# Head, rope weights and first post-norm of a decoder layer: a row tile in halves, low parts moved to GpSimd, scalings moved to ScalarE

## The chip, the cores and the metric

The kernel runs on one core of a Trainium2 chip. The metric is the device time of one execution in microseconds. The time of a kernel is the median over several executions; the profile comes from one further execution, whose own time is given beside its span.

The engines are named as the profile names them: TensorE is PE (its weight load is a row of its own, PEld), VectorE is DVE, ScalarE is ACT, GpSimd is POOL, SyncE is SP. Each engine takes its instructions in a fixed order, and a transfer is issued by an instruction in the queue of an engine.

## The reference

One decoder layer on 512 tokens of width 1024, all in float32:

```python
h = layer_norm(x, ln_in_g, ln_in_b)
proj = h @ w_in                       # q, k, v, r, gate rank, latents, branch gates
y_gla = (rms_norm(gla_chunked(q, k, v, log_a)) * silu(r)) @ w_o_gla
qm = rms_norm(q_lat) @ w_q_b          # 8 heads, each 128 plain + 64 rope columns
y_mla = merge(mla_causal_attention(...)) @ w_o_mla
mix = (g_gla * y_gla + g_mla * y_mla) @ w_out
h = layer_norm(alpha * h + mix, ln1_g, ln1_b)
ff = square(relu(h @ w_ff1)) @ w_ff2
return layer_norm(alpha * h + ff, ln2_g, ln2_b)
```

## The kernel before

**Precision.** A float32 operand is split into a high part, rounded to the type fp32r, and a low part, the rest. ACT writes the high part and DVE subtracts it to get the low part (`split`, L103 to L110). Each product is three matmuls, high by high, high by low and low by high: L230 to L232 in `gemm_fm`, which gives an output with features on the partitions, and L263 to L265 in `gemm_tm`, which gives tokens on the partitions.

**Weights.** All weights go through one stream of entries of up to 1024 columns in total. For each entry SP issues the transfers into `wraw` (three buffers), ACT converts it into `whi` (L179) and DVE subtracts for `wlo` (L180); `whi` and `wlo` have two buffers each. `pump` keeps the transfers two entries ahead of the products and the conversion one entry ahead. `plan` cuts a weight into entries of `per` blocks of 128 rows, two unless said otherwise. For the entries of the latent projection (`lat`, marked `res`) the parts have the names `xh` and `xl`, and they are converted ahead of their turn.

**Head.** `x` comes in four row tiles of 128 tokens. `load_x` (L117) puts their transfers on SP's queue: tile 0 in two halves of 512 columns, then tile 1 whole, both ahead of the first weights, tiles 2 and 3 later. `ln_rows` (L345) takes the statistics of a row tile in two halves (L348, DVE), aggregates them, adds the epsilon (L350), raises to the power -0.5 on POOL (L351) and normalises. For tile 0 that is done on ACT (L355) with a bias `nmr` that DVE works out (L354); for the others on DVE (L357). `ln_transpose` (L359) then goes over the eight blocks of 128 features: PE transposes the block for a pair of row tiles into PSUM (L366, two transposes), ACT scales and shifts it and rounds it to the high part `h` (L369), a second scaling of the same block gives `lnt` in full precision, and DVE subtracts for the low part (L374). The second scaling is on DVE (L373), or, with `alt`, on ACT for odd blocks (L371). `ln_in0` does this for row tiles 0 and 1 with `alt`, `ln_in1` for 2 and 3 without. Behind the first pair of tiles come the latent products of those tokens, token-major, then the same for the second pair, then q and k.

`last_in` is the low part of one block of the first pair. Some small DVE work of the head may be issued only after it. `lane_levels` begins with two copies of the lane masks into `cmask` (L910, DVE), which the GLA levels use much later.

**Middle.** The GLA levels run as a side lane beside the projections of v, r and of the branch gates. The gates are two groups of projections, and after each one `mla_qr` multiplies the normalised latent with the rope columns of four heads: 64 columns of each head of `w_q_b`, 256 columns, three blocks of 128 rows. `plan_qr` (L290) plans these weights with `per` = 2, so there are two entries for each group, one of two row blocks and one of one. The next entry behind the second group is the first one of `w_o_gla` for `y_gla`.

**First post-norm (LN1).** Behind the output projection `ln1` runs `ln_rows` and `ln_transpose` (without `alt`, name `h1`) for one pair of row tiles after the other; the second pair runs beside the first products of `w_ff1`, which use the first pair's tokens only.

**What sets the order.** The kernel's text yields from many generators, and a scheduler with its own model of the costs then fixes the order of the instructions on each engine. `tc.issue_after(x)` forbids an instruction to be issued ahead of x. So an edit in one place can move instructions of others on an engine. The profile's lines are those of the kernel before.

Of the kernel before, what the change touches and what calls it, by code (L numbers as in the profile page):

```python
# [16 lines left out]
ALU = mybir.AluOpType  # L17
AX = mybir.AxisListType

P = 128  # L20
T = 512
D = 1024
# [9 lines left out]
NOPE = 128  # L32
ROPE = 64
HQ = NOPE + ROPE
# [12 lines left out]
LEVELS = (1, 2, 4, 8, 16, 32, 64)  # L47
# [5 lines left out]
def tile_hybrid_block(ctx: ExitStack, tc: tile.TileContext, I, out, dbg=None):  # L53
    nc = tc.nc
# [17 lines left out]
    def A(shape, dt=F32, n="a"):  # L72
        tag, bufs = ("C", 8) if n in TAG_C else (n, TAG_W[n]) if n in TAG_W else ("A", 24)
        return pa.tile(shape, dt, tag=tag, bufs=bufs, name=nm(n))

    def B(shape, dt=F32, n="b"):
        return pb.tile(shape, dt, tag="B", name=nm(n))

    def S(shape, dt=F32, n="s"):
        return sm.tile(shape, dt, tag=n, name=nm(n))  # L80

    def MM(n="mm"):
        return pm.tile([P, T], F32, tag="mm", name=nm(n))

    def PX(shape=(P, T), dt=F32, n="px"):
        return px.tile(list(shape), dt, tag="px", name=nm(n))

    def f(ap):
        return ap.bitcast(F32)

    act = nc.scalar.activation
    vtt = nc.vector.tensor_tensor
    vts = nc.vector.tensor_scalar
    stt = nc.vector.scalar_tensor_tensor
    gtt = nc.gpsimd.tensor_tensor
# [21 lines left out]
    def load_x(*tts):  # L117
        for tt in tts:
            t = A([P, D], F32, "x")
            for c in (slice(0, T), slice(T, D)) if tt == 0 else (slice(0, D),):  # L120
                nc.sync.dma_start(t[:, c], I["x"][tt * P:(tt + 1) * P, c])
            xt.append(t)
    load_x(0, 1)
    ident = ca[:, 0:P]
    g_in = ca[:, P:P + NK]
# [8 lines left out]
    st = {"dma": 0, "spl": 0, "gates": ()}  # L134
    DMA_AHEAD, SPLIT_AHEAD = 2, 1

    def plan(name, c0, n, k_lo=0, k_hi=None, heads=None, res=False, per=2):
        w = I[name]
        K = w.shape[0] // P
        k_hi = K if k_hi is None else k_hi  # L140
        idx = []
        for k0 in range(k_lo, k_hi, per):
            nk = min(per, k_hi - k0)
            if heads is None:
                src = w.rearrange("(k p) n -> p k n", p=P)
                dmas = [(slice(0, nk), src[:, k0:k0 + nk, c0:c0 + n], None)]
            else:
                hw, h0, nh = heads
                src = w.rearrange("(k p) (h c) -> p k h c", p=P, c=hw)
                cw = n // nh  # L150
                dmas = [(kk, src[:, k0 + kk, h0:h0 + nh, c0:c0 + cw], cw) for kk in range(nk)]
            idx.append(len(stream))
            stream.append({"dmas": dmas, "nk": nk, "n": n, "res": res})
        return {"idx": idx, "nk": k_hi - k_lo, "per": per}

    def pump(i):
        while st["dma"] < min(len(stream), i + 1 + DMA_AHEAD):
            e = stream[st["dma"]]
            st["dma"] += 1
            if "src" in e:  # L160
                continue
            raw = A([P, e["nk"], T * 2 // e["nk"]], F32, "wraw")
            for sl, src, cw in e["dmas"]:
                dst = raw[:, sl, :e["n"]]
                if cw is not None:
                    dst = dst.rearrange("p (h c) -> p h c", c=cw)
                nc.sync.dma_start(dst, src)
            e["raw"] = raw
        while st["spl"] < min(len(stream), i + 2 + SPLIT_AHEAD):
            e = stream[st["spl"]]  # L170
            if st["spl"] > i + e.get("ahead", SPLIT_AHEAD) and not e["res"]:
                break
            nk, n = e["nk"], e["n"]
            hi, lo = [A([P, nk, T * 2 // nk], F32R, w) for w in HOME["a" if e["res"] else e.get("home", "w")]]
            raw = e["src"]() if "src" in e else e.pop("raw")
            with ExitStack() as gates:
                for g in st["gates"]:
                    gates.enter_context(tc.issue_after(g.ins))
                st["ins"] = act(hi[:, :nk, :n], raw[:, :nk, :n], AF.Copy)  # L179
                vtt(lo[:, :nk, :n], raw[:, :nk, :n], f(hi[:, :nk, :n]), op=ALU.subtract)  # L180
            st["gates"] = ()
            e["w"] = (hi, lo)
            st["spl"] += 1
# [33 lines left out]
    def part(x, i, c):  # L217
        return x[i][:, c] if isinstance(x, tuple) else x[:, i, c]
# [63 lines left out]
    PL = {}  # L282
# [5 lines left out]
        PL["v", hp] = plan("w_in", C_V + hp * T, T)  # L288
        PL["r", hp] = plan("w_in", C_R + hp * T, T)
    def plan_qr(g):  # L290
        PL["qr", g] = plan("w_q_b", NOPE, 4 * ROPE, heads=(HQ, 4 * g, 4))

    for br in range(2):
        for mb in range(2):
            PL["g", br, mb] = plan("w_in", C_G + br * D + mb * T, T)
        plan_qr(br)
# [48 lines left out]
    def ln_rows(src, dst, mv, on_act=False):  # L345
        bst = S([P, 2, 6], F32, "bst")
        for j in range(2):
            nc.vector.bn_stats(bst[:, j, :], src[:, j * T:(j + 1) * T])  # L348
        nc.vector.bn_aggr(mv, bst)
        vts(mv[:, 1:2], mv[:, 1:2], LN_EPS, None, op0=ALU.add)  # L350
        st["pow"] = gtt(mv[:, 1:2], mv[:, 1:2], mhalf[:, 0:1], op=ALU.pow)  # L351
        if on_act:
            nmr = S([P, 1], F32, "nmr")
            stt(nmr, mv[:, 0:1], -1.0, mv[:, 1:2], op0=ALU.mult, op1=ALU.mult)  # L354
            act(dst, src, AF.Identity, scale=mv[:, 1:2], bias=nmr)  # L355
        else:
            vts(dst, src, mv[:, 0:1], mv[:, 1:2], op0=ALU.subtract, op1=ALU.mult)  # L357

    def ln_transpose(rows, g, b, outs, hf, alt=False, n="h0"):  # L359
        tk = slice(hf * 256, (hf + 1) * 256)  # L360
        for k in range(NK):
            if len(outs) <= k:
                outs.append(A([P, 2, T], F32R, n) if n == "h0" else (B([P, T], F32R, n), B([P, T], F32R, n)))
            p = MM() if alt and k in (4, 5) else PX()
            for i in range(2):
                nc.tensor.transpose(p[:, i * P:(i + 1) * P], rows[2 * hf + i][:, k * P:(k + 1) * P], ident)  # L366
            tmp = B([P, 256], F32, "lnt")
            hi, lo = part(outs[k], 0, tk), part(outs[k], 1, tk)
            ha = act(hi, p[:, :256], AF.Identity, scale=g[:, k:k + 1], bias=b[:, k:k + 1])  # L369
            if alt and k % 2:  # L370
                act(tmp, p[:, :256], AF.Identity, scale=g[:, k:k + 1], bias=b[:, k:k + 1])  # L371
            else:
                vts(tmp, p[:, :256], g[:, k:k + 1], b[:, k:k + 1], op0=ALU.mult, op1=ALU.add)  # L373
            hd = vtt(lo, tmp, f(hi), op=ALU.subtract)  # L374
            if n == "h1":
                st["ln"] = (ha, hd)
            yield hd
# [4 lines left out]
    def ln_in0():  # L382
        for tt in range(2):
            ln_rows(xt[tt], xt[tt], mvin[:, tt, :], on_act=tt == 0)
        yield from ln_transpose(xt, g_in, b_in, hT, 0, alt=True)

    pump(-1)
    last_in = list(ln_in0())[3]


    act(identr, ident, AF.Copy)
# [7 lines left out]
    lmask = cmask.bitcast(U8)[:, :nl * 256].rearrange("p (l o u i) -> p l o u i", l=nl, o=2, u=2)  # L399
    lmi = A([P, 2, len(LEVELS), 64], I32, "lmi")  # L400
# [395 lines left out]
    def mla_pair(pr):  # L796
        vt = [None] * NT
        qn = [None] * 2
        kn = [None] * 2

        def ev_v(a, j, ps):
            t = B([P, 2, 256], F32R, "mv")
            split(ps[:, :256], t[:, 0, :], t[:, 1, :])
            vt[a] = t

        def ev_n(dst, sc):
            def e(a, ps):
                dst[a] = A([P, 2, T], F32R, "qn")
                split(ps, dst[a][:, 0, :], dst[a][:, 1, :], scale=sc)
            return e  # L810
        gemm_fm(PL["qn", pr], qlT, 256, ev_n(qn, scale))
        gemm_fm(PL["kn", pr], ckT, 256, ev_n(kn, None))
        return ([spawn(mla_head(2 * pr + a, a, qn[a], kn[a], vt)) for a in range(2)],
                lambda guard=None: gemm_tm([PL["mv", pr]], ckT, 256, ev_v, guard=guard))
# [92 lines left out]

    def lane_levels():
        for o in range(2):
            nc.vector.tensor_copy(lmask[:, :, o], lmi[:, o, :, None, :].to_broadcast([P, len(LEVELS), 2, 64]))  # L910
        for h in range(GH):
            yield from gla_levels(h)
            lv[h] = True

    def lane_out():
        for h in range(GH):
            yield from gla_out(h)

    t_lv, t_out = spawn(lane_levels()), spawn(lane_out())

    def levels_upto(h):
# [56 lines left out]
    t0, mv = mla_pair(0)  # L978
    mv()
    y_gla(1)  # L980
    t1, mv = mla_pair(1)
    mv(lambda: finish(*t0))
    t2, mv = mla_pair(2)
    mv(lambda: finish(*t1))
    t3, mv = mla_pair(3)
# [322 lines left out]
```

## Time and profile before

| | |
|---|---|
| median of 3 runs | 889.64 us (889.6, 889.64, 890.25) |
| the profiled execution's own time | 889.94 us |
| its span in the trace | 888.0 us, 11561 instructions |
| granted TensorE clock, mean | 0.996 |
| PE busy | 866.7 us, 98% of the span, 4352 matmuls |
| PE weight load busy | 738.3 us, 83% |
| DVE busy | 578.2 us, 65% |
| ACT busy | 432.7 us, 49% |
| POOL busy | 173.8 us, 20% |

The share of busy time is over the whole span. A row of the timeline gives the start in us from the span's start, the duration of the group, the engine, line, operation, and output and inputs; in square brackets stands the idle time ahead of it and what ended that. `x4` at its end means that four equal instructions in a row are shown as one row. A row of the waits gives who waited, for whom, the sum in us, the count and the mean. A row of the windows gives the stretch, its length with PE's busy time and count, the granted clock, the share of the transfer engines and their GB/s.

### The profile page before, as it was taken

To read this page: it belongs to the slowest core of one execution; us is meant where nothing else is said; L and a number is where in the kernel's file an instruction comes from. 1 tells how busy PE (TensorE), PEld (TensorE's weight loads), DVE (VectorE), ACT (ScalarE), POOL (GpSimd) and SP (SyncE) were. 2 spreads that over 40 slices of the span, in tenths; PEclk is the share of its full clock that TensorE was granted. 3 is DMA by queue.
4 is the path that set the end of the run, shared out by engine and by line. 5 is a ranking of instruction groups with operands and counts; after the bars stand their busy time and mean duration, and the time that the engine had idled before them with its cause. 6 is when DMAs were issued, how large, how long until landed. Compare 5 with 4: busy or idle time off the path is not lost.

```text
span 888.0 us, 11561 instructions
## 1 busy us (share of the span) xinstructions
PE 866.7 (98%) x4352; PEld 738.3 (83%) x4352; DVE 578.2 (65%) x987; ACT 432.7 (49%) x734; POOL 173.8 (20%) x211
## 2 busy tenths in 40 slices
PE   5999999999999999999999999999999999999995
PEld 5988888888888888889888888988888888888884
DVE  7834875667735234657766797997557646754687
ACT  5446453445434334435654423466357546645661
POOL 0303441434512010000000012104400520242022
PEclk9999999999999999999999999999999999999998
DMA  7513223221223232111307628006940991398075
GB/s 231 147 48 90 77 72 95 72 72 48 78 59 88 74 107 91 61 46 55 102 25 277 190 70 286 1 0 158 296 117 25 258 254 31 70 308 192 1 189 95
DMA packets 63270, 101.13 MB, mean 114 GB/s; under 512 B 7761, under 2 KB 31748, under 8 KB 63216
## 3 DMA queue, kind: packets, MB, share of 16 engines
q1 hardware_dynamic: 48256, 64.04, 23.4%
q0 software_dynamic: 13040, 32.71, 15.3%
q10 hardware_dynamic: 1920, 3.66, 1.2%
q8 instruction: 34, 0.56, 0.2%
q14 instruction: 20, 0.16, 0.1%
HBM read 82.56 MB, written 3.67 MB: 97 GB/s over the span
## 4 chain that ended last, share of the span: by engine, by line
PE 95%; DVE 2%; DMA 2%; issue 1%; ACT 0%; POOLq 0%; SPq 0%; POOL 0%; DVEq 0%; ACTq 0%
PE mm L230 16%; PE mm L232 16%; PE mm L231 16%; PE mm L263 5%; PE mm L265 5%; PE mm L264 5%; PE px L1153 3%; PE px L1155 3%; PE px L1154 3%; PE mm L1153 2%; PE mm L1155 2%; PE mm L1154 2%; PE px L690 1%; DMA x<-in_x_dram 1%; PE px L852 1%; PE px L265 1%
## 5 line engine op out<-in xcount | busy, mean ns | idle before, releaser
L180 DVE TENSOR_TENSOR wlo<-wraw,whi 128x1024 fp32r<-128x1024 f32 (+1 forms) x104 | 117.4, 1129 | 152.8 <-ACT whi L179 147.6
L230 PE MATMUL mm<-h,whi 128*128 128x512 f32 x416 | 162.8, 393 | 0.0
L231 PE MATMUL mm<-h,whi 128*128 128x512 f32 x416 | 162.2, 390 | 0.0
L179 ACT ACTIVATE whi<-wraw 128x1024 fp32r<-128x1024 f32 (+1 forms) x104 | 100.2, 963 | 122.2 <-PE mm L231 62.9
L232 PE MATMUL mm<-h,wlo 128*128 128x512 f32 x416 | 155.3, 390 | 0.0
L1181 POOL DMA_DIRECT2D res<-ev x54 | 47.8, 989 | 236.2 <-ACT ev L1179 196.4
L232 PEld LDWEIGHTS mm<-h,wlo 128*128 128x128 f32 x416 | 78.1, 188 | 16.3
L230 PEld LDWEIGHTS mm<-h,whi 128*128 128x128 f32 x416 | 78.1, 188 | 15.6
L231 PEld LDWEIGHTS mm<-h,whi 128*128 128x128 f32 x416 | 78.1, 188 | 15.6
L264 PE MATMUL mm<-wlo,h 128*128 128x512 f32 x128 | 50.6, 395 | 0.0
L265 PE MATMUL mm<-whi,h 128*128 128x512 f32 x128 | 50.3, 394 | 0.0
L263 PE MATMUL mm<-whi,h 128*128 128x512 f32 x128 | 49.9, 400 | 0.0
L1235 ACT ACTIVATE relu<-mm 128x512 f32<-128x512 f32 x32 | 18.8, 595 | 57.3 <-PE mm L232 57.3
L351 POOL TENSOR_TENSOR mv<-mv,mhalf 128x1 f32<-128x1 f32 x4 | 5.5, 1385 | 209.2 <-DVE mv L350 209.2
L616 POOL TENSOR_TENSOR rp<-rp 128x256 f32<-128x256 f32 x32 | 29.9, 936 | 63.6 <-ACT E L634 52.8
L641 DVE TENSOR_TENSOR M<-E,qk 128x256 f32<-128x256 f32 x48 | 28.9, 629 | 12.4 <-ACT E L634 12.2
L634 ACT ACTIVATE E<-rp 128x512 f32<-128x512 f32 x32 | 20.4, 638 | 26.2 <-POOL rp L617 26.1
L179 ACT ACTIVATE xh<-wraw 128x1024 fp32r<-128x1024 f32 (+1 forms) x20 | 18.9, 959 | 26.9 <-PE mm L265 15.5
L180 DVE TENSOR_TENSOR wlo<-wq,whi 128x1024 fp32r<-128x1024 f32 x15 | 18.4, 1224 | 19.7 <-ACT whi L179 19.7
L265 PEld LDWEIGHTS mm<-whi,h 128*128 128x128 f32 x128 | 24.1, 188 | 4.8
L264 PEld LDWEIGHTS mm<-wlo,h 128*128 128x128 f32 x128 | 24.1, 188 | 4.5
L263 PEld LDWEIGHTS mm<-whi,h 128*128 128x128 f32 x128 | 24.0, 188 | 4.2
(381 smaller groups left out, 2235.2 us busy)
## 6 DMA issues: line engine op xcount, KB each, us to landing
wraw<-in_w_in_dram SPq DMA_DIRECT2D x40, 512.0 KB, 3.7
wraw<-in_w_ff_dram SPq DMA_DIRECT2D x32, 512.0 KB, 8.0
wq<-in_w_ff_dram POOLq DMA_DIRECT2D x32, 512.0 KB, 9.3
res<-ev POOLq DMA_DIRECT2D x54, 256.0 KB, 8.8
wraw<-in_w_o_gla_dram SPq DMA_DIRECT2D x8, 512.0 KB, 3.7
wraw<-in_w_o_mla_dram SPq DMA_DIRECT2D x8, 512.0 KB, 3.3
wraw<-in_w_out_dram SPq DMA_DIRECT2D x8, 512.0 KB, 4.2
wraw<-in_w_in_dram SPq DMA_DIRECT2D x8, 360.0 KB, 4.6
```

What stands on the lines that cost most here:

```text
L179: st["ins"] = act(hi[:, :nk, :n], raw[:, :nk, :n], AF.Copy)
L180: vtt(lo[:, :nk, :n], raw[:, :nk, :n], f(hi[:, :nk, :n]), op=ALU.subtract)
L230: mm(o, hi[:, c], xh, start=first, stop=False)
L231: mm(o, hi[:, c], xl, start=False, stop=False)
L232: mm(o, lo[:, c], xh, start=False, stop=last)
L263: mm(o, xh, hi[:, :n], start=opens, stop=False, skip_group_check=share)
L264: mm(o, xh, lo[:, :n], start=False, stop=False, skip_group_check=share)
L265: mm(o, xl, hi[:, :n], start=False, stop=last, skip_group_check=share)
L1153: mm(o, xh[:, c], hi[:, pp, cols], start=opens, stop=False, skip_group_check=True)
L1154: mm(o, xh[:, c], lo[:, pp, cols], start=False, stop=False, skip_group_check=True)
L1155: mm(o, xl[:, c], hi[:, pp, cols], start=False, stop=hf == 1 and pp == 1, skip_group_check=True)
L1181: nc.gpsimd.dma_start(res[tt + t][:, j * T:(j + 1) * T], e, accum_op=ALU.add)
```

## The change

There are four edits.

1. In the head, row tile 1 is loaded in two halves like tile 0. The second half's statistics of tile 1 may be issued only after tile 0's `nmr`.
2. In the head, for the four odd blocks of row tiles 0 and 1, where ACT does the second scaling, POOL subtracts for the low part instead of DVE. `last_in` becomes the low part of the fifth block instead of the fourth, and the two lane mask copies wait for it too.
3. A group's rope weights become one entry of three row blocks (`per` = 4). The three transfers stay as they are.
4. In LN1 the second scaling of odd blocks is done by ACT instead of DVE. The low part stays on DVE there.

```diff
-            for c in (slice(0, T), slice(T, D)) if tt == 0 else (slice(0, D),):
+            for c in (slice(0, T), slice(T, D)) if tt < 2 else (slice(0, D),):
                 nc.sync.dma_start(t[:, c], I["x"][tt * P:(tt + 1) * P, c])
...
     def plan_qr(g):
-        PL["qr", g] = plan("w_q_b", NOPE, 4 * ROPE, heads=(HQ, 4 * g, 4))
+        PL["qr", g] = plan("w_q_b", NOPE, 4 * ROPE, heads=(HQ, 4 * g, 4), per=4)
...
     def ln_rows(src, dst, mv, on_act=False):
         bst = S([P, 2, 6], F32, "bst")
         for j in range(2):
-            nc.vector.bn_stats(bst[:, j, :], src[:, j * T:(j + 1) * T])
+            with ExitStack() as after:
+                if j and "nmr" in st:
+                    after.enter_context(tc.issue_after(st.pop("nmr").ins))
+                nc.vector.bn_stats(bst[:, j, :], src[:, j * T:(j + 1) * T])
...
-            stt(nmr, mv[:, 0:1], -1.0, mv[:, 1:2], op0=ALU.mult, op1=ALU.mult)
+            st["nmr"] = stt(nmr, mv[:, 0:1], -1.0, mv[:, 1:2], op0=ALU.mult, op1=ALU.mult)
...
-            if alt and k % 2:
+            if k % 2 and (alt or n == "h1"):
                 act(tmp, p[:, :256], AF.Identity, scale=g[:, k:k + 1], bias=b[:, k:k + 1])
             else:
                 vts(tmp, p[:, :256], g[:, k:k + 1], b[:, k:k + 1], op0=ALU.mult, op1=ALU.add)
-            hd = vtt(lo, tmp, f(hi), op=ALU.subtract)
+            hd = (gtt if alt and k % 2 else vtt)(lo, tmp, f(hi), op=ALU.subtract)
...
-    last_in = list(ln_in0())[3]
+    last_in = list(ln_in0())[4]
...
         for o in range(2):
-            nc.vector.tensor_copy(lmask[:, :, o], lmi[:, o, :, None, :].to_broadcast([P, len(LEVELS), 2, 64]))
+            with tc.issue_after(last_in.ins):
+                nc.vector.tensor_copy(lmask[:, :, o], lmi[:, o, :, None, :].to_broadcast([P, len(LEVELS), 2, 64]))
```

## Prediction

> **What bounds the kernel now.** I read the page's head and its chain first, then who TensorE (PE) waited for, then the stretches, and last the timeline at each place where PE stood still.
>
> ```profile
> PE 95%; DVE 2%; DMA 2%; issue 1%; ACT 0%; POOLq 0%; SPq 0%; POOL 0%; DVEq 0%; ACTq 0%
> ```
> ```profile
> PE px L366 <- ACT x L355: 9.0, 1, 9.0
> ...
> PE mm L263 <- ACT h L369: 0.8, 1, 0.8
> ...
> PE mm L265 <- DVE h L374: 0.7, 1, 0.7
> ...
> PE mm L232 <- DVE wlo L180: 0.5, 1, 0.5
> ...
> PE mm L230 <- ACT h L369: 0.3, 1, 0.3
> ```
> ```profile
> 870.00:888.00 18.00, 8.18 (x47) 0.82 0.63 117
> ```
>
> 95% of the chain that ended last is PE. The second view is the waits of PE: 9.0 us before its first instruction, and four short ones, 2.3 us together. The third gives PE's busy time at the end: 8.18 of 18 us, so 9.8 us of tail. The change touches no matmul and no instruction of the tail. It can only shorten the start, the four waits and what is hidden between matmuls, so its reach is about 3 us in the span. The profiled execution took 889.94 us, 0.30 above the median of the runs shown (889.64); I sum on 889.94 and take the 0.30 off at the end. A difference under 0.2%, 1.8 us, is what a measurement of this kernel can hardly tell from none.
>
> **Part 1, the second row tile in halves.** Rows picked from the timeline, as in the fences of the later parts (the transfer's row is from the chain in order of time; PEld is PE's weight load):
>
> ```profile
> 1.65 5.25 DMA x<-in_x_dram
> ...
> 4.19 1.53 DVE L348 BATCH_NORM_STATS2 bst<-x 128x6 f32<-128x512 f32 x2 [3.31 <-DMA x<-in_x_dram]
> ...
> 6.23 0.56 POOL L351 TENSOR_TENSOR mvin<-mvin,mhalf 128x1 f32<-128x1 f32 x1 [5.78 <-DVE mvin L350]
> ...
> 6.92 0.69 DVE L348 BATCH_NORM_STATS2 bst<-x 128x6 f32<-128x512 f32 x1 [0.77 <-DMA x<-in_x_dram]
> ...
> 7.53 0.14 DVE L354 SCALAR_TENSOR_TENSOR nmr<-mvin 128x1 f32<-128x1 f32 x1
> ...
> 7.71 1.24 ACT L355 ACTIVATE x<-x,nmr,mvin 128x1024 f32<-128x1024 f32 x1 [3.05 <-DVE nmr L354]
> ...
> 9.00 1.11 PE L366 MATMUL px<-ca,x 128*128 128x128 f32 x4 [9.00 <-ACT x L355]
> ```
>
> GpSimd (POOL) has tile 0's power ready at 6.23 + 0.56 = 6.79. The tiny nmr that needs it stands on VectorE (DVE) behind the first statistics of tile 1, which wait for a 512 KB transfer until 6.90 (1.65 + 5.25). So nmr starts at 7.53, ScalarE (ACT) normalises at 7.71 and PE starts at 9.00. In halves, tile 0 began its statistics at 4.19, so half a tile lands well ahead of a whole one: if the 512 KB land evenly between tile 0's end (its second statistics began at 4.19 + 1.53 - 0.69 = 5.03) and 6.90, the first half is there at about 5.95. Its statistics then run from 6.10 to 6.79, inside POOL's power. nmr starts at 6.83, ACT at 7.01, PE at 8.31: **0.69 earlier**. The order of the changed program holds the second statistics behind nmr, so nothing queues ahead of it. The bounds are 0 (the first half lands only with the second) and 0.70 (nmr right behind the power). Added is one DMA issue on SP ahead of the weights, cost within the third rival. Tile 1's own chain begins at the same 6.92 with one statistics less to do, and comes 0.67 sooner as well.
>
> **Part 2, low parts of odd blocks on POOL, one lane mask copy later.**
>
> ```profile
> 8.79 0.56 POOL L351 TENSOR_TENSOR mvin<-mvin,mhalf 128x1 f32<-128x1 f32 x1 [2.00 <-DVE mvin L350]
> ...
> 12.82 0.68 DVE L910 CAST cmask<-lmi 128x896 uint8<-128x896 int32 x1
> ...
> 13.88 0.58 ACT L371 ACTIVATE lnt<-px,ca 128x256 f32<-128x256 f32 x1
> ...
> 15.14 1.42 DVE L374 TENSOR_TENSOR h<-lnt,h 128x256 fp32r<-128x256 f32 x4
> ...
> 15.94 0.60 PE L265 MATMUL mm<-xh,h 128*128 128x360 f32 x2 [0.66 <-DVE h L374]
> ...
> 16.37 0.61 ACT L371 ACTIVATE lnt<-mm,ca 128x256 f32<-128x256 f32 x1
> ...
> 17.24 0.69 DVE L348 BATCH_NORM_STATS2 bst<-x 128x6 f32<-128x512 f32 x1 [0.53 <-DMA x<-in_x_dram]
> ...
> 19.71 1.09 DVE L374 TENSOR_TENSOR h<-lnt,h 128x256 fp32r<-128x256 f32 x3
> ...
> 20.18 0.30 PEld L265 LDWEIGHTS mm<-xh,h 128*128 128x128 f32 x2 [0.32 <-DVE h L374]
> ...
> 22.86 0.90 DVE L180 TENSOR_TENSOR xl<-wraw,xh 128x720 fp32r<-128x720 f32 x1
> ...
> 23.02 1.14 POOL L351 TENSOR_TENSOR mvin<-mvin,mhalf 128x1 f32<-128x1 f32 x1 [13.21 <-DVE mvin L350]
> ```
> ```profile
> L710 POOL TENSOR_TENSOR sd<-SD,sd 128x256 fp32r<-128x256 f32 x4 | 2.9, 734 | 12.8 <-ACT sd L709 12.8
> ```
>
> PE stood at 15.94 and 20.18 for low parts of odd blocks. Their scaled values were on ACT's side by 13.88 + 0.58 = 14.46 and 16.37 + 0.61 = 16.98, but DVE was busy: with the mask copy (0.68) before the first, and, before the second, with statistics that waited for row tile 2. Now POOL takes them. The last view groups a POOL subtraction of the very same shape: 0.73 us, against 1.42 / 4 = 0.36 on DVE. First block: scaled at 14.46 - 0.69 = 13.77, low part at about 13.82 + 0.73 = 14.55. PE would be there at 15.94 - 0.66 - 0.69 = 14.59. So alone on its port POOL is just in time.
>
> It is not alone: DVE does two low parts just then. The row for that is POOL's power, 0.56 at 8.79 and 1.14 at 23.02, beside a DVE subtraction of two tensors. The Trainium skill, SBUF — State Buffer, "Who interferes with whom", says why: a DVE instruction with two SBUF inputs contends with a GpSimd instruction that reads SBUF, and whichever issued first keeps the port for its whole instruction. By that rule the trace agrees (0.58 longer), and the price here is one whole DVE instruction.
>
> I put one DVE low part (0.36) ahead of POOL's: ready at 14.91, PE there until about 14.95, so 0.99 gained instead of 0.69. The bounds are one 0.90 subtraction in front (15.45, gain 0.49) and nothing (14.59, gain 1.35). Second block: scaled at 16.98 - 0.69 = 16.29, low by 17.1 to 18.0, while PE arrives at 20.18 - 0.32 - 0.99 = 18.87. That wait goes: gain 1.31 so far. What is late next: the weights' low parts behind row tile 2's statistics on DVE, which start 0.69 sooner because SP's queue (the transfer is issued when DVE frees a weight buffer) shifts as a whole.
>
> **Part 3, what the new order does to the second half of the head.** In the changed order ACT converts one 1024-wide weight entry, then does four blocks, and only then the next entry; row tile 3's transposes stand on PE ahead of 22 matmuls instead of behind them.
>
> ```profile
> 27.25 0.93 DVE L357 TENSOR_SCALAR x<-x,mvin 128x1024 f32<-128x1024 f32 x1 [0.44 <-POOL mvin L351]
> ...
> 28.91 1.06 ACT L179 ACTIVATE whi<-wraw 128x1024 fp32r<-128x1024 f32 x1 [3.04 <-DMA wraw<-in_w_in_dram]
> ...
> 30.00 1.23 DVE L180 TENSOR_TENSOR wlo<-wraw,whi 128x1024 fp32r<-128x1024 f32 x1 [1.81 <-ACT whi L179]
> ...
> 30.41 1.06 ACT L179 ACTIVATE whi<-wraw 128x1024 fp32r<-128x1024 f32 x1 [0.44 <-DMA wraw<-in_w_in_dram]
> ...
> 31.73 1.93 ACT L369 ACTIVATE h<-px,ca 128x256 fp32r<-128x256 f32 x4
> ...
> 32.34 0.43 PE L263 MATMUL mm<-xh,h 128*128 128x360 f32 x1 [0.82 <-ACT h L369]
> ...
> 33.09 0.99 DVE L373 TENSOR_SCALAR lnt<-px,ca 128x256 f32<-128x256 f32 x2
> ```
>
> PE was free at 32.34 - 0.82 = 31.52 and waited because the block (31.73) stood behind the second entry, which waited for its transfer until 30.41. Now it stands behind the first alone: 28.91 + 1.06, less some 0.7 to 1.3 of earlier transfer, plus one block (1.93 / 4 = 0.48): 29.2 to 29.8. PE comes at 31.52 - 1.31 = 30.21. The 0.82 goes: gain 2.13. But DVE now does the entry's 1.23 subtraction before three scalings (0.99 / 2 = 0.5 each) and a low part (0.36): 3.1 behind that conversion, done between 31.8 and 32.4. PE needs that low part after four matmuls and six transposes, at about 31.5 (1.3 us of work behind 30.21, an estimate from the counts). So a wait of 0.3 to 0.9 appears. I take 0.4, of which half stood hidden in before too: net +0.2. The head gives **1.95**, bounds 0.9 and 2.9.
>
> **Part 4, rope weights as one entry.**
>
> ```profile
> 321.61 1.06 ACT L179 ACTIVATE whi<-wraw 128x1024 fp32r<-128x1024 f32 x1 [1.98 <-PE mm L265]
> ...
> 323.19 2.89 DVE L180 TENSOR_TENSOR wlo<-wraw,whi 128x1024 fp32r<-128x1024 f32 x2
> ...
> 324.46 0.74 PE L232 MATMUL mm<-ogT,wlo 128*128 128x512 f32 x2 [0.51 <-DVE wlo L180]
> ```
>
> The first GLA output entry could be converted only when the first rope entry's buffer came free (321.61), and its low part fell behind the rope arithmetic on DVE. With one entry for the three row blocks, that conversion takes the buffer which the last gate entry frees, before the rope matmuls begin, some 3 us sooner. The 0.51 wait goes; the same three DMAs are issued, and the following entry's conversion has an entry's 24 matmuls as cover. **0.5**, bounds 0.2 and 0.51. The other group had no wait to lose.
>
> **Part 5, odd blocks of LN1 scaled on ACT.**
>
> ```profile
> 559.64 2.84 ACT L369 ACTIVATE h<-px,cb 128x256 fp32r<-128x256 f32 x6 [4.33 <-PE px L366]
> ...
> 560.24 1.00 DVE L373 TENSOR_SCALAR lnt<-px,cb 128x256 f32<-128x256 f32 x2 [0.76 <-ACT h L369]
> ...
> 561.63 0.38 PE L231 MATMUL mm<-h,xh 128*128 128x256 f32 x1
> ```
>
> The 0.3 wait ends with ACT's first block at 559.64 + 0.47; nothing ahead of it changes, so it stays. Behind it DVE has one scaling instead of two before the first low part: PE's first use of it moves from 561.63 to about 561.28, but one pair of transposes (some 0.2) moves behind that. **0.1**, bounds 0.3 gained and 0.2 lost: ACT's scalings follow four blocks, to about 562.0, and PE wants their low part near 563.4 (12 matmuls and six transposes, 2.1 us, behind 561.28; an estimate). DVE's time saved over 8 blocks lies beside PE and pays nothing.
>
> **Sum.** 1.95 + 0.5 + 0.1 = 2.55; 889.94 - 2.55 = 887.4, and with the 0.30 off, **887.1**. Bounds of the parts together: 886.0 to 888.7.
>
> **The rivals.** *A, DVE and POOL get in each other's way:* each of the four POOL subtractions waits for a 0.90 one of DVE or holds one up. The first wait then stays (gain 0.49), Part 3's new wait is 0.7, and the later weights come late. Head 1.0, total about 1.3: 888.3. For it speaks the row at 23.02; against it that PE has over 0.8 us to spare at the other three. *B, row tile 3 too early on PE:* if its normalisation still ends where it did (27.25 + 0.93 = 28.18), PE, which would reach the transposes near 25.8, idles 2.4 us and meets the four blocks no sooner than before: the head's gain is used up, about 889.1. Against it: in the new order that step no longer stands behind a weight subtraction, and I get its end at 24.9 to 25.9. *C, slower:* the same place, if row tile 3 comes still later, since the extra DMA moves every later transfer one slot down in SP's queue and in the rotation of completion marks, and a weight load may wait for a mark that it did not wait for before. From 30.6 on for the normalisation's end the kernel is slower than before by 1.8 us, 891.4; it would need a transfer 2.4 us later than in before, and I see 1.7 us at most of later issue, of one weight entry whose place in the full queue hides it. *D:* the first half lands only with the second: Part 1 is worth 0 and the total 1.9, 887.8.
>
> **How the numbers follow.** Forecast 0.60, D 0.06 (just faster), A 0.15 (a fifth of it faster), B 0.11 and C 0.08. Faster by over 0.2%: 0.60 + 0.06 + 0.03 = 0.69; within: 0.12 + 0.11 = 0.23; slower: 0.08. The range is the bounds of the sum, up to A's upper end: 886.0 to 888.9.
>
> **What would show it.** PE's first transpose near 8.3; no wait of PE on the low part near 19, none on ACT near 30, none at 322; a wait of some 0.4 on DVE near 31.5; POOL's four subtractions at 0.7 to 1.6 us; the 0.3 at LN1 still there. Wrong, if PE waits over 1 us for row tile 3's normalisation, or if POOL's first low part ends after 15.5.

## The result, and the profile after

| | before | changed |
|---|---|---|
| median of 22 runs each, us | 890.47 | 888.75 |
| lowest and highest, us | 889.01, 893.76 | 888.12, 889.61 |
| profiled execution and its span, us | 889.94, 888.0 | 889.34, 887.4 |

The ratio is 0.9977, with a 95% interval of 0.9970 to 0.9984: 2.0 us faster, between 1.4 and 2.7. The median lies 1.7 us under that of before. The forecast was 887.1 with a range of 886.0 to 888.9, so the time is inside the range, at its upper end. The two profiled executions differ by 0.6 us only; the second profile of the kernel before, below, shows why.

The waits of TensorE (PE) in the changed kernel, in us in total, times, longest; then its last stretch:

```profile
PE px L369 <- ACT x L358: 8.5, 1, 8.5
PE mm L265 <- POOL h L377: 0.5, 1, 0.5
PE mm L264 <- DVE xl L180: 0.4, 1, 0.4
PE px L369 <- DVE x L360: 0.4, 1, 0.4
PE mm L230 <- ACT h L372: 0.3, 1, 0.3
```
```profile
870.00:888.00 18.00, 7.22 (x43) 0.83 0.64 117
```

The lines have moved by three: L369 is the old L366, L377 the old L374. The waits on ACT's block (0.8), on DVE's low part (0.7) and on the GLA output weights (0.5) are gone. Three new ones have come: on GpSimd's (POOL's) low part, on a weight's low part from DVE, and on row tile 1. The 0.3 at LN1 stayed, as forecast. PE ends 0.96 us earlier than in before (8.18 less 7.22 of busy time in that stretch).

The head of the changed kernel, rows picked from the timeline:

```profile
6.45 0.69 DVE L351 BATCH_NORM_STATS2 bst<-x 128x6 f32<-128x512 f32 x1 [0.37 <-DMA x<-in_x_dram]
...
7.06 0.14 DVE L357 SCALAR_TENSOR_TENSOR nmr<-mvin 128x1 f32<-128x1 f32 x1
...
7.82 0.69 DVE L351 BATCH_NORM_STATS2 bst<-x 128x6 f32<-128x512 f32 x1 [0.61 <-DMA x<-in_x_dram]
...
8.53 1.12 PE L369 MATMUL px<-ca,x 128*128 128x128 f32 x4 [8.53 <-ACT x L358]
...
9.61 0.81 DVE L360 TENSOR_SCALAR x<-x,mvin 128x1024 f32<-128x1024 f32 x1 [0.67 <-POOL mvin L354]
...
10.48 1.12 PE L369 MATMUL px<-ca,x 128*128 128x128 f32 x4 [0.41 <-DVE x L360]
...
14.61 2.53 POOL L377 TENSOR_TENSOR h<-lnt,h 128x256 fp32r<-128x256 f32 x2 [5.04 <-ACT lnt L374]
...
14.62 0.75 DVE L377 TENSOR_TENSOR h<-lnt,h 128x256 fp32r<-128x256 f32 x2
15.28 0.72 DVE L419 TENSOR_SCALAR hbg<-cb 128x16 f32<-128x16 f32 x1
...
16.03 0.60 PE L265 MATMUL mm<-xh,h 128*128 128x360 f32 x2 [0.53 <-POOL h L377]
...
18.55 1.29 DVE L351 BATCH_NORM_STATS2 bst<-x 128x6 f32<-128x512 f32 x2 [1.87 <-DMA x<-in_x_dram]
...
22.04 0.43 PE L264 MATMUL mm<-xl,h 128*128 128x360 f32 x1 [0.42 <-DVE xl L180]
...
28.80 1.06 ACT L179 ACTIVATE whi<-wraw 128x1024 fp32r<-128x1024 f32 x1 [2.09 <-DMA wraw<-in_w_in_dram]
...
29.77 1.92 ACT L372 ACTIVATE h<-px,ca 128x256 fp32r<-128x256 f32 x4
...
31.66 1.06 ACT L179 ACTIVATE whi<-wraw 128x1024 fp32r<-128x1024 f32 x1
```

In the kernel before, tile 1's normalisation was this row:

```profile
9.38 0.98 DVE L357 TENSOR_SCALAR x<-x,mvin 128x1024 f32<-128x1024 f32 x1 [0.67 <-POOL mvin L351]
```

Three things are to be seen. First, PE starts 0.47 sooner (8.53), but tile 1 is normalised at 9.61 + 0.81 = 10.42, and was at 9.38 + 0.98 = 10.36 before: PE stands still at 10.48 and the lead is gone. Second, POOL's first two low parts take 2.53 us together, beside two of DVE's, and PE goes on at 16.03, where it was 15.94. Third, ACT converts one weight entry, does four blocks (29.77) and only then the second entry, and no PE wait is left there.

### The profile page after: what moved, and what is told of

Same layout as the page of the kernel before. It is cut to its first block, busy times and chain, and to the rows that moved or that the text cites. A ratio compares the mean times of both kernels' runs of the same rounds, so it can differ in the third digit from the quotient of the medians.

```text
span 887.4 us, 11559 instructions
## 1 busy us (share of the span) xinstructions
PE 866.8 (98%) x4352; PEld 738.7 (83%) x4352; DVE 573.3 (65%) x973; ACT 435.0 (49%) x740; POOL 172.5 (19%) x215
## 4 chain that ended last, share of the span: by engine, by line
PE 90%; DVE 4%; DMA 4%; ACT 1%; issue 1%; POOL 0%; POOLq 0%; DVEq 0%; SPq 0%; ACTq 0%
PE mm L230 16%; PE mm L231 15%; PE mm L232 15%; PE mm L265 5%; PE mm L264 5%; PE mm L263 5%; PE px L1157 3%; PE px L1159 3%; PE px L1158 3%; PE mm L1157 2%; PE mm L1158 2%; PE mm L1159 2%; PE px L693 1%; DVE xl L180 1%; DMA wraw<-in_w_out_dram 1%; PE px L855 1%
## 5 line engine op out<-in xcount | busy, mean ns | idle before, releaser
L180 DVE TENSOR_TENSOR wlo<-wraw,whi 128x1024 fp32r<-128x1024 f32 (+2 forms) x102 | 117.0, 1147 | 156.1 <-ACT whi L179 149.8
L179 ACT ACTIVATE whi<-wraw 128x1024 fp32r<-128x1024 f32 (+2 forms) x102 | 99.9, 979 | 126.2 <-PE mm L231 64.9
```

## The experiments

Each run has 9 to 12 executions, beside 31 to 35 of the kernel before on the same chip. Half a microsecond in a median is near what that can tell, so the main readings are taken from the traces, at one point of the work: how much earlier (-) or later (+) the k-th matmul or transpose of PE starts than in the first profile of before. (Own table, from the starts in the traces.) At the 61st and the 151st the changed order has one or two transposes in other places than before, which is worth some 0.1 there; from the 261st on the same work lies ahead of each point in all kernels.

| kernel | 1st | 11th | 61st | 151st | 261st | 1501st | 1751st | 3001st | median, us |
|---|---|---|---|---|---|---|---|---|---|
| before, second profile | 0.01 | 0.01 | 0.71 | 1.26 | 1.26 | 1.26 | 1.23 | 1.25 | 890.29 |
| rope entry alone (head as before) | -0.26 | -0.26 | 0.71 | 0.36 | 0.36 | 0.57 | -0.28 | -0.28 | 889.43 |
| changed, first profile | -0.47 | 0.07 | 0.53 | -1.01 | -0.56 | -0.36 | -1.20 | -0.96 | 888.75 |
| changed, second | -0.45 | 0.14 | 0.18 | -0.79 | -0.37 | -0.19 | -1.04 | -1.16 | 889.01 |
| changed, third | -0.47 | 0.34 | 0.66 | -0.66 | -0.25 | -0.05 | -0.89 | -1.01 | 888.45 |
| LN1 edit undone | -0.29 | 0.34 | -0.09 | -1.40 | -0.98 | -0.78 | -1.62 | -0.99 | 888.89 |
| tile 1 whole | 0.13 | 0.00 | -0.70 | 1.75 | 2.09 | 2.29 | 1.44 | 1.33 | 890.51 |
| tile 1 whole, ACT's order kept | 0.06 | -0.07 | -0.43 | -1.02 | -0.69 | -0.50 | -1.35 | -1.45 | 888.73 |
| all low parts on DVE | -0.42 | -0.20 | -0.27 | -1.23 | -0.59 | -0.39 | -1.23 | -1.33 | 889.33 |
| two low parts on POOL | -0.48 | 0.19 | -0.30 | -1.85 | -1.44 | -1.23 | -2.08 | -2.19 | 888.68 |
| the same, tile 1 whole, both statistics late | -0.40 | 0.72 | 0.10 | -0.90 | -0.83 | -0.65 | -1.49 | -1.60 | 888.07 |
| the same again | -0.65 | 0.64 | -0.01 | -0.96 | -0.54 | -0.36 | -1.21 | -1.32 | 888.51 |
| two on POOL, tile 1's normalisation in halves | -0.29 | 0.16 | 0.70 | -0.71 | -0.30 | -0.13 | -0.98 | -1.09 | 888.84 |

The 261st lies behind the head, the 1501st ahead of the second rope group, the 1751st behind it, the 3001st behind LN1.

**The kernel before again.**

> The kernel before, unchanged, for a second profile and the spread of its times. Theory M (what the medians say beyond the traces comes from waits of TensorE in the head that are longer in other executions of the kernel before): the ratio is 1.000 within 0.0005, and where the profiled execution's own time is over 890.3 its waits in the first 36 us sum to at least 0.5 us more than the 11.3 us of the first profile. Rival N (the executions differ without waits, in TensorE's pitch or in the tail behind its last matmul): waits of 11.2 to 11.5 us again whatever the time; the pitch of the latent products behind 37.5 us, 160 ns in the first profile, or the tail of 9.8 us, moves instead.

The ratio was 0.9993 (0.9980 to 1.0006), 0.0002 outside the band of Theory M; its profiled execution took 891.01. The waits of PE and of its weight load in its head:

```profile
20.89 0.30 PEld L265 LDWEIGHTS mm<-xh,h 128*128 128x128 f32 x2 [1.02 <-DVE h L374]
20.89 0.60 PE L265 MATMUL mm<-xh,h 128*128 128x360 f32 x2 [0.72 <-DVE h L374]
...
33.60 0.43 PE L263 MATMUL mm<-xh,h 128*128 128x360 f32 x1 [1.36 <-ACT h L369]
```
```profile
29.54 1.06 ACT L179 ACTIVATE whi<-wraw 128x1024 fp32r<-128x1024 f32 x1 [3.05 <-DMA wraw<-in_w_in_dram]
31.67 1.06 ACT L179 ACTIVATE whi<-wraw 128x1024 fp32r<-128x1024 f32 x1 [1.08 <-DMA wraw<-in_w_in_dram]
```

Theory M holds for this execution: the same two waits grew (by the weight load's rows 0.32 to 1.02, by PE's 0.82 to 1.36), and all 1.26 us of the difference arise in the head; from the 151st matmul to the end the two profiles of before differ by a constant within 0.03. The second wait is the one that the forecast named: ACT's block stands behind the second entry, whose transfer came 1.26 later here (31.67 against 30.41). The first profile of before was thus a lucky one, and the difference of the first two profiles (0.6) too small.

**The changed kernel again, twice.**

> The changed kernel, unchanged, for a second profile. The ratio to before is 0.997 to 0.999. If the late landings of its first profile (weight entry at 17.17 instead of 15.81, row tile 2 at 18.52 instead of 17.22) belong to the extra transfer they come again within 0.3 us; if they are chance, they land by 16.1 and 17.5, the 0.4 us wait for the weights' low part goes, and the second half of the head starts 0.5 us sooner. If the pitch of 165 ns behind 37.5 us belongs to the changed order it comes again; if chance, it is 160.

> The changed kernel a third time, on the chip of the two candidates, for the comparison. 888.4 to 889.2, ratio 0.9975 to 0.9990. Theory (GpSimd's first low part, not the clock or a transfer, sets TensorE's stop in the first half): it takes 1.2 to 1.4 us again and TensorE goes on at 15.9 to 16.2, whenever the full clock came. Rival: it takes under 1.0 us where the clock comes late.

Ratios 0.9989 (0.9975 to 1.0003) and 0.9979 (0.9970 to 0.9988). The late landings are chance at least in part: row tile 2's statistics began at 18.55, 17.84 and 18.66 in the three profiles. POOL's first low part was no chance. It took 1.37 us in all three, while the first matmul at full clock came between 13.8 and 15.2, and PE went on at 16.03, 16.09 and 16.30, each time as POOL ended. So POOL sets that stop. (16.30 is 0.1 over the expectation: there tile 1 was normalised later, and PE's second transposes began at 10.75 instead of 10.48.) The pitch of 165 ns came again (below).

**Row tile 1 whole.**

```diff
-            for c in (slice(0, T), slice(T, D)) if tt < 2 else (slice(0, D),):
+            for c in (slice(0, T), slice(T, D)) if tt == 0 else (slice(0, D),):
```

> The changed kernel with row tile 1 loaded whole again. Theory (the halves gain nothing, because TensorE's next need is tile 1's normalisation, and that came no sooner, 10.42 against 10.36): first transpose at 8.9 to 9.1, no wait for tile 1 behind it, the 11th matmul within 0.1 us of 11.35, the first weight entries land 0.6 us sooner; time within 0.3 us of the changed kernel. Rival (the prediction's step: the halves are worth their 0.47 to 0.69): 0.5 to 0.7 us slower than the changed kernel, and everything behind the head stands that much later.

Neither. The first half of the head was as the theory says, and better than with the halves: start 9.13, the 11th at the same place, the 61st 0.70 ahead of before. Then came a loss of 2.6 us between the 111th and the 151st, which the expectation didn't have. ACT in this kernel, PE's wait, and PE by stretches (length, busy, count, granted clock, share of the transfer engines, GB/s):

```profile
30.32 1.06 ACT L179 ACTIVATE whi<-wraw 128x1024 fp32r<-128x1024 f32 x1 [1.17 <-DMA wraw<-in_w_in_dram]
31.28 1.91 ACT L372 ACTIVATE h<-px,ca 128x256 fp32r<-128x256 f32 x4
```
```profile
31.88 0.43 PE L263 MATMUL mm<-xh,h 128*128 128x360 f32 x1 [1.18 <-ACT h L372]
```
```profile
30.58:33.98 3.40, 1.85 (x9) 1.00 0.87 227
33.98:37.40 3.42, 3.42 (x12) 0.50 0.43 145
37.40:40.80 3.40, 3.40 (x24) 1.00 0.00 0
```

ACT has before's order again: both entries, then the blocks. Nothing in the halves touches ACT there; the scheduler, with other times at the start, chose otherwise. (In the runs further below with tile 1 whole and both its statistics late, the changed kernel's order came back.) Behind the stop one stretch of 3.42 us ran at half the clock, 1.7 us of work lost. The Trainium skill, TensorE: Matmul & The Clock Gate, Part 1, puts the fall back to half clock behind an idle window of about 3.4 us. In this trace the window ahead of it was not idle: PE was busy 1.85 of 3.40 us. Five steps of 3.41 us lie between the doubling of the clock (13.53) and the start of that window. In the second profile of before the stop was longer (1.36), but in the window as many steps behind the doubling there (15.11), 32.18 to 35.59, PE was busy 2.03 us, and the clock stayed full. In four of the five executions of the kernel with tile 1 whole that took over 891.5 us the mean granted clock was 0.995, in the six under 890.6 it was 0.996 or 0.997. So probably some had such a stretch and some not, and the median is no measure of the wait alone.

**The same, with ACT's order held.**

```diff
+            if n == "h0" and hf == 1 and k == 3:
+                st["h3"] = ha
             yield hd
...
             with ExitStack() as gates:
+                if st["spl"] == 9:
+                    gates.enter_context(tc.issue_after(st["h3"].ins))
```

> The changed kernel with row tile 1 whole (as in the run without the halves), and one order added: the conversion of the second 1024-wide weight entry may be issued only after the fourth block of the second pair of row tiles, as the changed kernel has it. TensorE's order is that of the run without the halves. Theory (ACT's order is what the halves brought, through the scheduler): the 1.2 us wait near 32 for an ACT block shrinks under 0.3, no window of half clock follows it, the profile stands 0.8 to 1.1 us ahead of the kernel before at the 150th matmul, and the times are 888.3 to 889.3 without a second group near 892. Rival (TensorE's own order, row tile 3's transposes late, is what costs): the wait moves to those transposes, the times stay at 889.1 to 890.5 and 891.7 to 892.4, in two groups.

888.73 (ratio 0.9982, 0.9974 to 0.9991), all between 888.07 and 889.64, and the wait is gone from the list:

```profile
PE px L371 <- ACT x L360: 9.1, 1, 9.1
PE mm L267 <- POOL h L379: 0.9, 1, 0.9
PE mm L232 <- ACT h L374: 0.3, 1, 0.3
```

PE's order is that of the run with tile 1 whole but for one pair of transposes. The theory holds, with a range of times a little wider than forecast. At the 261st matmul the two traces lie 2.78 us apart, of which 1.7 are the stretch at half clock (half of 3.42); the other 1.1 are worth as much as the whole head of the change, and they come as well without the halves.

**Low parts on POOL: none, two.**

```diff
-            hd = (gtt if alt and k % 2 else vtt)(lo, tmp, f(hi), op=ALU.subtract)
+            hd = vtt(lo, tmp, f(hi), op=ALU.subtract)
```

> The changed kernel with the four odd low parts on VectorE again, the other edits kept. Theory (GpSimd's first two subtractions, 1.37 and 1.20 us, came because VectorE subtracts at the same time, and moved the wait from VectorE to GpSimd): the first odd low part ends between 15.0 and 15.5 instead of 15.98, the 0.5 us wait there shrinks to under 0.2 because the mask copy is out of the way, but the second place waits again, 0.2 to 0.5; the sum is within 0.3 us of the changed kernel. Rival (GpSimd's help is what gains): waits of 0.7 and 0.3 as in the kernel before, and 0.5 to 1.0 us slower than the changed kernel.

889.33 (ratio 0.9990, 0.9980 to 1.0000), 0.3 above the changed kernel on that chip (889.01). PE's first stop ended at 15.15 instead of 16.09, but it still lasted 0.68, since the full clock came early (12.1) and so did PE; the second place waited 0.56. Summed, the 61st matmul is 0.45 ahead of the second profile of the changed kernel, the 261st 0.22. So the theory's main point holds as far as these show: POOL's help on the first two blocks gains nothing. The later mask copy had no run of its own.

```diff
+            hd = (gtt if alt and k in (5, 7) else vtt)(lo, tmp, f(hi), op=ALU.subtract)
```

> The changed kernel with GpSimd's low parts for the sixth and eighth block only; the second and fourth go back to VectorE. Theory (GpSimd is slow where VectorE subtracts beside it, and quick behind): TensorE's first stop ends at 15.2 instead of 16.0, its second place does not stop, GpSimd's two subtractions take 0.73 to 0.9 us each; the 60th matmul stands 0.6 to 0.9 us ahead of the kernel before instead of 0.2 to 0.5 behind, and the time is 0.4 to 0.9 us under the changed kernel: 887.9 to 888.6. Rival (VectorE is full there, so its two low parts hold up the weights' low parts): a stop of 0.5 to 0.9 for those near 21, the same time as the changed kernel.

888.68, ratio 0.9980 (0.9972 to 0.9989); in the trace 1.0 to 1.2 us ahead of the changed kernel's three at the 3001st, the best of all profiles; in time within 0.35 of the changed kernel's three medians, which the measurement cannot tell apart. DVE and POOL there:

```profile
14.73 1.09 DVE L377 TENSOR_TENSOR h<-lnt,h 128x256 fp32r<-128x256 f32 x3
...
18.89 0.89 DVE L180 TENSOR_TENSOR xl<-wraw,xh 128x720 fp32r<-128x720 f32 x1
```
```profile
17.25 0.74 POOL L377 TENSOR_TENSOR h<-lnt,h 128x256 fp32r<-128x256 f32 x1 [7.25 <-ACT lnt L374]
18.86 1.52 POOL L377 TENSOR_TENSOR h<-lnt,h 128x256 fp32r<-128x256 f32 x1 [0.86 <-ACT lnt L374]
```

DVE does three low parts in 1.09 and PE does not stop there. POOL's first stands alone: 0.74, the price of the forecast's row. Its second began 0.03 ahead of a DVE subtraction of two tensors by the trace, and took 1.52, 0.78 longer; the expectation's 0.73 to 0.9 missed it. The 61st matmul was 0.30 ahead of before and not 0.6 to 0.9: PE waited 0.27 near 21 for a weight's low part, a small form of the rival's stop.

**The early start without the extra transfer, and a finer normalisation.**

```diff
-                if j and "nmr" in st:
-                    after.enter_context(tc.issue_after(st.pop("nmr").ins))
+                if "nmr" in st:
+                    after.enter_context(tc.issue_after(st["nmr"].ins))
+                    if j:
+                        st.pop("nmr")
```

(with tile 1 whole and two low parts on POOL)

> As the run with two low parts on GpSimd, with row tile 1 whole and both its statistics behind tile 0's nmr: the early start without the extra transfer. Theory (the start is set by the order on VectorE, and weights and row tile 2 land sooner without the extra transfer): first transpose at 8.3 to 8.6, tile 1's transposes at 10.3 to 10.4, first weight entries at 8.2 to 8.3, the 60th matmul 0.8 to 1.1 us ahead of the kernel before; time 887.6 to 888.5. Rival (the halves make tile 1 land sooner and that counts): 0.3 to 0.6 us slower than the run with the halves.

> Two low parts on GpSimd, row tile 1 whole, both its statistics behind tile 0's nmr, beside the changed kernel on one chip. Theory (no wait of the head is long any more, so late transfers cost little): 887.8 to 888.7, 0.3 to 0.9 us under the changed kernel, all runs within 1 us. Rival (its 1.0 us wait for tile 1's normalisation, behind a weight subtraction on VectorE, eats what the low parts give): within 0.2 us of the changed kernel.

888.07 (ratio 0.9977, 0.9967 to 0.9986) and 888.51 (0.9977, 0.9968 to 0.9986). PE starts at 8.60 and 8.35, so the order alone gives the start. But it waits 1.0 and 1.1 us for tile 1, whose normalisation now stands behind a weight subtraction on DVE, and at the 61st it is level with before (0.10 and -0.01) instead of 0.8 to 1.1 ahead. Beside the changed kernel on one chip (888.45) it is no better: the rival holds. No version here beats the changed kernel measurably.

```diff
-            vts(dst, src, mv[:, 0:1], mv[:, 1:2], op0=ALU.subtract, op1=ALU.mult)
+            cs = (slice(0, T), slice(T, D)) if dst is xt[1] else (slice(0, D),)
+            for c in cs:
+                vts(dst[:, c], src[:, c], mv[:, 0:1], mv[:, 1:2], op0=ALU.subtract, op1=ALU.mult)
```

(with the halves and two low parts on POOL)

> Two low parts on GpSimd, row tile 1 in halves as in the change, and its normalisation on VectorE in two halves of 512 columns. Theory (TensorE's second transposes wait for the end of a normalisation of which they need the first half only): the 0.5 us wait there goes to under 0.15 and the 11th matmul comes 0.4 us sooner than in the run with the whole normalisation (11.5); up to 0.4 less in the end if the weights' low parts at 21 don't give it back. Rival (they do): the wait near 21 grows from 0.3 to 0.6 or more and the time is that of the run before, 888.7 within 0.3.

888.84 (ratio 0.9981, 0.9972 to 0.9991). The wait went from 0.54 to 0.32 only, and the one at 22 was 0.70: the rival holds. What is won at the start is given back where row tile 2 and the weights land.

**The rope entry alone.**

```diff
-        PL["qr", g] = plan("w_q_b", NOPE, 4 * ROPE, heads=(HQ, 4 * g, 4))
+        PL["qr", g] = plan("w_q_b", NOPE, 4 * ROPE, heads=(HQ, 4 * g, 4), per=4)
```

> The kernel before with the rope weights as one entry, nothing else. Theory (the prediction's step, with what the changed kernel's traces show): up to 200 us as the kernel before, 0.1 to 0.3 us lost by 300, then the 0.5 us wait at 324 gone and 0.8 gained, so 0.5 to 0.7 less from 340 to the end; ratio 0.9990 to 0.9998. Rival (the wait only moves to the next entry of the GLA output weights): a new wait of 0.3 to 0.5 between 325 and 345, and nothing gained.

889.43, ratio 0.9993 (0.9985 to 1.0001), too little for the times to show, but by the trace just as expected: 0.21 lost by the 1501st, 0.85 gained by the 1751st, 0.64 net, and then nothing more. The same two steps, within 0.04, are in each profile that has this edit. ACT's conversion of the first GLA output entry, in the second profile of the changed kernel:

```profile
318.45 1.05 ACT L179 ACTIVATE whi<-wraw 128x1024 fp32r<-128x1024 f32 x1
```

It was at 321.61: 3.2 us sooner, as forecast. The rival's new wait is in no list.

**LN1's scalings on DVE again.**

```diff
-            if k % 2 and (alt or n == "h1"):
+            if alt and k % 2:
```

> The changed kernel with all LN1 scalings on VectorE again. Theory (the prediction's step: the edit is worth 0.1): between the 2500th and the 3000th matmul the distance to the kernel before changes by less than 0.03 us, where the changed kernel gained 0.12 in its second profile; the wait of 0.3 us near 560 is there in both. Rival (the loss of 0.25 there in the changed kernel's first profile belongs to the edit): undone, it is gone, and the second profile was the exception. The time is within 0.3 us of the changed kernel either way.

888.89 (ratio 0.9982, 0.9974 to 0.9991), 0.4 above the changed kernel on that chip, and the trace went against both: from the 1751st to the 3001st it lost 0.63, where the second and third profile of the changed kernel gained 0.12 and the first lost 0.24. PE and DVE there:

```profile
546.30 0.36 PE L230 MATMUL mm<-h,xh 128*128 128x256 f32 x1 [0.36 <-DVE res L1016]
```
```profile
540.33 1.23 DVE L180 TENSOR_TENSOR wlo<-wraw,whi 128x1024 fp32r<-128x1024 f32 x1 [2.40 <-ACT whi L179]
```

With PE 1.62 ahead, this weight subtraction on DVE began 0.26 ahead of before's (540.59): it had to wait for its entry. Behind it stands LN1's chain of scalings and low parts, and then the sum that frees the accumulator which PE needs for the first product of the next stage. So in this profile a gain made elsewhere was given back here. From that subtraction to the sum the chain has four scalings and took 5.14 us; with the scalings on ACT it has two and took 4.64 in the second profile of the changed kernel, where it began at 539.60 and PE did not wait, and 4.31 in the first, where it began at 541.10 and PE lost 0.24 all the same.

Both profiles that lost time here had a late transfer. ACT converted the entry in before, without the LN1 edit and in the first profile of the changed kernel at:

```profile
539.49 1.06 ACT L179 ACTIVATE whi<-wraw 128x1024 fp32r<-128x1024 f32 x1 [1.51 <-DMA wraw<-in_w_ff_dram]
```
```profile
539.24 1.06 ACT L179 ACTIVATE whi<-wraw 128x1024 fp32r<-128x1024 f32 x1 [2.56 <-DMA wraw<-in_w_ff_dram]
```
```profile
540.01 1.06 ACT L179 ACTIVATE whi<-wraw 128x1024 fp32r<-128x1024 f32 x1 [2.58 <-DMA wraw<-in_w_ff_dram]
```

With PE 1.62 and 1.20 ahead there, that is 1.37 and 1.72 us later beside PE's work than in before. The next latest, 1.09, with the edit (tile 1's normalisation in halves), gained 0.11. So one profile without the edit cannot tell the edit's part from the transfer's, and 0.4 in the medians is near what the times can tell: that the edit saved 0.63 is not shown.

## Why the prediction was right, and where its steps were not

The total holds: 2.55 were forecast, 1.7 (medians) to 2.0 (ratio) measured, and the sign. There is luck in it. Of the 1.65 us between the forecast and the time, 0.83 is the base: 889.64 was the median of three runs, that of 22 is 890.47. The time lies above the upper end of the sum's own bounds (888.7) and 0.15 inside the range, whose end was A's; a repeat of the changed kernel had 889.01. Whether it is faster by over 0.2% stays open: 0.23% by the ratio, 0.19% by the medians. And the sum came about otherwise. To weigh the parts I use the table, with the mean of the three profiles with before's head (first, second, rope entry alone) and of the four with the changed one (three of the changed kernel, LN1 undone). At the 261st these spread by 1.26 and 0.73, so a difference of the two means is good to some 0.4.

*Part 1 failed as a step.* 0.69 at the start was 0.47 in the first profile and 0.34 by the means; at the 11th matmul the changed kernel is 0.31 behind. The first half's statistics began at 6.45 instead of 6.10. I let tile 1's chain begin with its second half at 6.90 and "come 0.67 sooner as well". The second half was there at 7.82, so the normalisation ended at 10.42 instead of 10.36. In two transfers the tile took longer than in one; I had put the extra transfer to the third rival and not into tile 1's own chain.

*Part 2 went the way of rival A.* I put one DVE low part (0.36) ahead of POOL's 0.73. POOL took 1.37 for the first, beside two low parts of DVE. The Trainium skill, SBUF — State Buffer, "Who interferes with whom", lets the instruction issued first block the other for its whole length. With that rule the traces agree in kind, 0.74 alone and up to 1.52 beside DVE, but not always in the order: by their starts POOL's was the first of the two, at 14.61 and at 18.86, and it was the one held up. It held DVE up in turn: DVE's next instruction (`hbg`, 15.28) took 0.72, where it took 0.17 in before, and ended with POOL's low part (16.00 and 15.98). With tile 1 whole DVE began first by 0.02 (14.51 and 14.53), and POOL's first low part took 0.97. "Wrong, if POOL's first low part ends after 15.5", the prediction said: it ended at 15.98. At the 61st matmul the gain is 0.47 - 0.32 = 0.15 instead of 1.31.

*Part 3 was right and too small.* Its wait on ACT's block was 0.82 in the first profile of before, and 0.47 and 1.36 in the other two; in the four of the changed head it is gone. From the 61st to the 151st the gain rises from 0.15 to 1.50 (0.54 less -0.96), by 1.35 where I had 0.64 (1.95 less 1.31; 2.13 less 0.2 would be 1.93); some 0.1 of it comes of the transposes that stand in other places. The wait that I put on DVE near 31.5 came in none of them, and row tile 3's early transposes (rivals B and C) cost nothing.

*Missed: the pitch.* From the 151st to the 261st the changed head gives 0.43 back without any wait, and before's head nothing: some 0.3 by matmuls 164 instead of 160 ns apart (some 66 of them), some 0.1 by those transposes. It leaves **1.08** for the head, against 1.95, within the bounds of 0.9 to 2.9.

*Part 4* was 0.64 for 0.5. Behind the second group 0.85 was gained, by the mechanism named. The wait's row said 0.51, but by the starts PE lost more there. Before's row ahead of that wait:

```profile
323.55 0.40 PE L231 MATMUL mm<-ogT,whi 128*128 128x512 f32 x1
```

The next matmul started at 324.46, 0.91 later, where with the rope entry alone that step took 0.23: 0.68 lost. The wait's row counts only from the end of the matmul ahead (323.55 + 0.40 = 323.95), and matmuls overlap when none waits. That the other group had nothing to lose was wrong by 0.2, lost without a wait and most of it between 263 and 285 us, around that group's products, where PE's order differs.

*Part 5* was 0.12 for 0.1 in two profiles of three, and 0.10 or 0.11 in all seven variants that keep the edit. Whether the rest of it "pays nothing beside PE" stays open: the one profile without the edit lost 0.63, with a late transfer.

Sum: 1.08 + 0.64 + 0.12 = 1.84. PE's end to the span's end took 9.8 us in three profiles with the head of before, and 9.95 to 10.24 in four of the changed one, which takes some 0.3 off in these profiles; in the seven others it took 9.61 to 9.95, so it does not come with the change. No instruction there differs and I have no cause for it. Of the cases, A's head of 1.0 is nearest to the 1.08, and in the first half it was A's mechanism; but A's later wait did not come, and its total of 1.3 is less than its head and Parts 4 and 5 give (1.6). By the gain alone the nearest is D's 1.9, whose mechanism it was not: the first half of the tile landed well ahead of the second.

## What to carry to other kernels

Where an engine's queue mixes work that waits for transfers with work that another engine waits for, put the second kind first: one conversion moved behind four blocks was worth 1.1 us between two profiles here, more than any of the finer cuts, and no wait of PE on that transfer's lateness was left. A single profile of a kernel with such a wait may be a lucky one; take a second before summing against it, and read what a wait cost from the starts on both sides of it. And follow a step that is cut in pieces to its last piece: a tile whose halves arrive sooner and later than the whole has the later half on the path.

## What the runs showed of the hardware

The same 128x360 matmuls ran at two pitches without a wait. Before, and then the changed kernel, ten matmuls each from the first to the last row, nine steps apart:

```profile
39.91 0.32 PE L265 MATMUL mm<-xh,h 128*128 128x360 f32 x1
...
41.35 0.32 PE L265 MATMUL mm<-xh,h 128*128 128x360 f32 x1
```
```profile
38.22 0.33 PE L265 MATMUL mm<-xh,h 128*128 128x360 f32 x1
...
39.70 0.66 PE L265 MATMUL mm<-xh,h 128*128 128x360 f32 x3
```

That is 160 and 164 ns. One pitch holds for tens of matmuls and changes at a stop or a transpose. The order of the instructions alone does not set it: the kernel with two low parts on POOL, tile 1 whole and both statistics late ran this stretch at 160 ns in its first profile and at 164 in its second. What sets it was not tried.

The doubling of the granted clock after the start came between 2.8 us (11.88 with 9.06, tile 1 whole and ACT's order kept) and 6.8 us (15.33 with 8.52, two low parts on POOL) after PE's first instruction. It differs between executions of one kernel too: 13.74, 14.95 and 15.17 in the three profiles of the changed one. There the next stop swallowed the difference (PE went on at 16.09, 16.03 and 16.30).
